# Two-layer hybrid decoder trunk on one core: layer 2's norm factors on four columns, layer 1's out projection with a block between, gate slices and y by four tiles

## The chip, the cores and the metric

The kernel runs on one core of a Trainium2 chip. The time is what the device takes for one execution of the whole program, in microseconds (us). A core has five engines with an instruction queue each: TensorE (PE; its weight loads are listed apart, as PEld), VectorE (DVE), ScalarE (ACT), GpSimd (POOL) and SyncE (SP), which here only issues DMAs. Each runs its queue in order, and waits on semaphores of the others. Matmuls write to PSUM, all else lies in SBUF or in DRAM. "Granted clock" is the TensorE clock that the throttle allowed, 1.00 being full speed.

## The reference

1024 tokens of width 1024, two layers. Layer 1 is forgetting attention (FoX: causal attention of 16 heads of 64 with a decay added to the scores), layer 2 three dilated window attentions whose results are mixed by their log-sum-exp. What bears on this change is the frame around the two mixers:

```python
def rms_norm(x, g):
    return x * lax.rsqrt(jnp.mean(x * x, axis=-1, keepdims=True) + EPS) * g

def fox_mixer(h, w_in, b_f, q_g, k_g):
    proj = h @ w_in
    q, k, v = ...                      # q and k normed by head
    gate = proj[..., 3 * INNER:4 * INNER]
    c = jnp.cumsum(jax.nn.log_sigmoid(f_logit), axis=1)
    return fox_attention(q, k, v, c), gate

for i in range(DEPTH):                 # DEPTH = 2: FoX, then dilated windows
    h = rms_norm(x, norm_g[i])
    o, gate = fox_mixer(h, ...) if i == 0 else dsw_mixer(h, ...)
    x = x + (o * jax.nn.silu(gate)) @ w_out
```

All is float32, and each large product is made of three f16 matmuls (high times high, high times low, low times high part), which keeps its accuracy.

## The kernel before, in words

**Layer 1's attention** goes by head pair (`hp`, 8 of them, two heads of 64 side by side) and query tile (`t`, 8 of 128 tokens). `fox_tile` writes one such tile: `score` makes the scores in PSUM, from which DVE makes p, ACT the exponentials and the transposed f16 parts (`ptt`, through a DMA); `values` multiplies by V into `o`; `finish` divides and gates: `rec` is the reciprocal of the softmax sum, and y = o * rec * gate for each of the two heads (L1158). The gates were projected at the start of the program and lie in DRAM (`gs_d`). In `score`, each tile loads its gate slice, 128 tokens by 128 columns (`gsf`, L1106), and `finish` stores y of the same shape to `y_d` (L1162). `turn_y` later loads rows of `y_d` back (`yt`) and PE transposes them (`transpose_rows`) for the out projection: k tiles 0 to 3, then 4 to 6. The last head pair's y (k tile 7) goes from SBUF to a transposition of its own (`turn_last`; L729 on PE, then ACT's cast to xh, L734, and DVE's remainder xl, L735).

**Layer 1's out projection** is `project_t`: the result is transposed, 128 output columns by 512 tokens in one PSUM tile `pj`. The 1024 columns come in three parts (`PARTS`, h = 0, 1, 2 with 384, 256 and 384 columns, so 3, 2 and 3 tiles m of 128), the tokens in two blocks b of 512. One such tile, a unit here, is 24 matmuls: 8 k tiles by 3. In part 0 the three units of a block are interleaved, with k tiles 0 to 3 first, then 4 to 6, then 7. Each part has a weight block of its own (`next_block` plans its loads, its bound, its scale and its `split` into f16 parts; the split's DVE step is L660, 128x768, 4 per block, one of which can go to POOL). Part 0 of both blocks stands between the last attention tiles; parts 1 and 2 follow.

**What is done with a unit** is `grown`: load the input's tile `xr`, add the projection times its weight scale (L1241), store the new x (`x1_d`) and the new x times layer 2's gain (`xn_d`), and add its square to `sacc`, by ACT, POOL and for the last unit of a block DVE. After a block's eighth unit `factors` makes layer 2's norm factor of its 512 tokens: one f32 matmul with a matrix of ones, 128x512, sums the squares over the partitions and leaves the sum in every row (`so`, L1262); DVE and ACT make 1/sqrt of it on all 128x512 values, in `fv` and `fy` in SBUF. `take` loads two tiles of `xn_d` back, multiplies by the factor (`xs`, L1275, DVE), casts to xh (ACT) and subtracts to xl (L1280, DVE for one and POOL for the other), and stores `xs` for later. Layer 2's gate projection (L694) reads xh and xl, block 0's tokens first. L904 is DVE's `peak` there, which reads the projected gates from PSUM.

**What sets the order.** The Python code says which instruction comes when in ticks: `flow.tick()` advances while matmuls are written, and `flow.at(tick, f)` writes work in at a tick; `CFG` holds the ticks for the weights' steps (`out`, `gate`), for `take` and for others. On top of it `plan_engines` and `order_engines` write a fixed order for each engine from a model of the durations: PE keeps the order of the program as far as the model calls its operands ready, DVE, ACT, POOL and SP go by the latest start that the model gives. On the chip each engine then takes that order as it is.

**Buffers.** `ps_pj` and `ps_s` have 3 PSUM tiles each, `ps_o` has 2. `n2k` is a tag of 2 KB tiles with `nb` = 3 buffers, used by `xr`, by the squares and gains of layer 1's beginning and the like; `gsl` has 3 gate slices in layer 1, `qs` 5 buffers.

Of the kernel before, what the change touches and what calls it, by code (L numbers as in the profile page):

```python
# [437 lines left out]
def trunk(ctx, tc, ins, out, cfg):  # L438
# [260 lines left out]
    def project_t(seq, done):  # L699
# [2 lines left out]
        todo = []
        for b, h in seq:
            n = PARTS[h][1] // P
            ms = [[m] for m in range(n)] if h else [list(range(n))]
            for mm in ms:
                for ks in [range(KT)] if h else [range(4), range(4, KT - 1), range(KT - 1, KT)]:
                    todo.extend((b, h, m, k) for m in mm for k in ks)
        n, s0 = 4 * NT * len({h for _, h in seq}), flow.now
        ps, ws = {}, {}  # L710
        for i, (b, h, m, k) in enumerate(todo):
            if h == 0:
                assert all((t, (k > 3) + (k > 6)) in turned for t in range(4 * b, 4 * b + 4)), (b, k, turned)
            if h not in ws:
                ws[h] = next_block(*cfg["out"][len(seq) > 2, len(ws)])
            if k == 0:
                ps[m] = ps_pj.tile([P, 512], F32, name="pj", tag="pj")
            for x, (j, a) in enumerate(((0, yh), (0, yl), (1, yh))):
                nc.tensor.matmul(ps[m], ws[h].slab(k, j)[:, m * P : (m + 1) * P], a[:, k, 512 * b : 512 * (b + 1)], start=(k == 0 and x == 0), stop=(k == KT - 1 and x == 2))  # L719
# [369 lines left out]

    def fox_tile(hp, t, kts, vt, sl):  # L1090
# [11 lines left out]
        def score(e, c):  # L1102
            a, b = pieces[c]
            if e == 0 and c == 0:
                gs = st["gs"] = lay([P, P], F32, name="gsf", tag="gsl")
                nc.sync.dma_start(gs, gs_d[t * P : (t + 1) * P, hp * P : (hp + 1) * P])  # L1106
# [45 lines left out]
        def finish():  # L1152
# [3 lines left out]
            y = sb.tile([P, P], F32, name="y", tag="y")  # L1156
            for e in range(2):
                nc.vector.scalar_tensor_tensor(y[:, e * HD : (e + 1) * HD], o[:, e, :HD], rec[:, e : e + 1], st["gs"][:, e * HD : (e + 1) * HD], ALU.mult, ALU.mult)  # L1158
# [100 lines left out]
    def factors(b):  # L1259

        so = ps_o.tile([P, 512], F32, name="so", tag="o")
        nc.tensor.matmul(so, ones.bitcast(F32), acc[:, b], start=True, stop=True)  # L1262
# [302 lines left out]
```

## Time and profile before

| | us |
|---|---|
| time, median of 3 runs | 1655.86 (1652.52 to 1656.51) |
| the profiled execution | 1656.83 |
| its span in the trace | 1654.8 |
| PE busy | 1605.9 |
| DVE busy | 1192.6 |
| ACT busy | 1063.5 |
| POOL busy | 963.9 |

The span is from the first to the last instruction of the profiled execution. Busy times are sums over an engine's instructions, by the trace; in a row of the trace x is a count, and `[0.74 <-DMA ptt<-ph]` says that the engine stood idle for 0.74 us ahead of this row, and that what it waited for last was the DMA that writes `ptt` from `ph`. `out<-in` are the program's names of the tiles, without their numbers. A name can be the buffer's: y (in `transpose_rows` the row to transpose) is `y` before the change. A row in the view by stage shows a stretch of time, the busy time of each engine in it (with the count of instructions), the granted clock, the share of the 16 DMA engines, and GB/s.

### The profile page before, as it was taken

How to read it: one execution, taken by the hardware profiler on the slowest of the kernel's cores; microseconds unless marked ns; L12 is line 12 of the kernel's file. 1: busy time of each engine (PE TensorE's matmuls, PEld its weight loads, DVE VectorE, ACT ScalarE, POOL GpSimd, SP SyncE). 2: the span in 40 equal slices, each digit the busy share in tenths (PEclk: the TensorE clock that was granted, in tenths of full speed). 3: DMA queues.
4: the chain of work that ended last, by engine and by line, in shares of the span. 5: the costliest groups of instructions: out<-in, count | busy, mean ns of one | idle time of the engine just before them, and what ended most of it. 6: DMA issues, size and time to landing. Idle time of an engine off the chain costs nothing.

```text
span 1654.8 us, 37873 instructions
## 1 busy us (share of the span) xinstructions
PE 1605.9 (97%) x13342; PEld 1037.5 (63%) x13342; DVE 1192.6 (72%) x3663; ACT 1063.5 (64%) x2746; POOL 963.9 (58%) x1252
## 2 busy tenths in 40 slices
PE   6999999999998999999999999999999999999999
PEld 4766667777664456566666666666666666666644
DVE  7757878888786586576767787777677877768751
ACT  7656778878776476566766687566566665666630
POOL 7315778778765241255555666667576766858430
PEclk9999999999999999999999999999999999999999
DMA  7335999999999884257876796768787586767952
GB/s 257 127 107 121 205 205 216 203 208 197 206 220 218 237 250 153 85 138 151 168 150 149 164 227 147 174 158 181 160 164 165 141 191 155 170 160 167 219 166 96
DMA packets 646479, 288.66 MB, mean 174 GB/s; under 512 B 493825, under 2 KB 610561, under 8 KB 646289
## 3 DMA queue, kind: packets, MB, share of 16 engines
q1 hardware_dynamic: 646288, 286.25, 74.5%
q8 instruction: 104, 1.70, 0.4%
q14 instruction: 87, 0.70, 0.1%
HBM read 124.35 MB, written 41.22 MB: 100 GB/s over the span
## 4 chain that ended last, share of the span: by engine, by line
PE 74%; DVE 10%; DMA 6%; ACT 4%; issue 3%; POOL 2%; SPq 0%; DVEq 0%; POOLq 0%; ACTq 0%
PE pj L694 56%; PE pj L719 7%; PE s L870 6%; DMA qk_t<-hl 3%; DVE w L660 2%; DVE p L1125 1%; PE ob L929 1%; PE ob L927 1%; PE ob L928 1%; DMA ptt<-ph 1%; ACT w L659 1%; PE o L929 1%; PE o L927 1%; PE o L928 1%; DVE xl L1280 1%
## 5 line engine op out<-in xcount | busy, mean ns | idle before, releaser
L694 PE MATMUL pj<-w,xh 128*128 128x384 f16 (+2 forms) x4864 | 1172.9, 324 | 6.0 <-DVE peak L904 4.3
L694 PE MATMUL pj<-w,xl 128*128 128x384 f16 (+2 forms) x2432 | 787.8, 324 | 5.2 <-DVE xl L1280 3.6
L694 PEld LDWEIGHTS <-xh 128*128 128x128 f16 x4864 | 468.1, 98 | 282.2 <-issue 8.2
L694 PEld LDWEIGHTS <-xl 128*128 128x128 f16 x2432 | 238.2, 98 | 157.5 <-DVE xl L1280 5.3
L1363 POOL TENSOR_TENSOR ph<-p,ph 128x768 f16<-128x768 f32 (+2 forms) x96 | 157.7, 1642 | 137.6 <-ACT ph L1362 130.1
L919 POOL TENSOR_TENSOR ph<-p,ph 128x512 f16<-128x512 f32 (+3 forms) x176 | 173.0, 1003 | 56.9 <-issue 37.5
L837 POOL TENSOR_TENSOR hl<-u,hl 128x512 f16<-128x512 f32 x128 | 150.9, 1179 | 53.6 <-ACT hl L836 44.9
L719 PE MATMUL pj<-xh,w 128*128 128x512 f16 x512 | 157.7, 381 | 6.2 <-DVE xr L1241 2.8
L870 PE MATMUL s<-qk_t 128*128 128x128 f16 (+1 forms) x1248 | 151.2, 238 | 6.8 <-DMA qk_t<-hl 5.1
L660 DVE SCALAR_TENSOR_TENSOR w<-raw,sws,w 128x768 f16<-128x768 f32 x96 | 146.6, 1528 | 11.0 <-ACT w L659 10.7
L794 ACT ACTIVATE sq<-pj 128x256 f32<-128x256 f32 x256 | 96.4, 377 | 86.5 <-DVE u L789 85.7
L789 DVE TENSOR_TENSOR u<-pj,gr 128x256 f32<-128x256 f32 x256 | 106.9, 418 | 45.8 <-PE pj L694 44.0
L913 ACT ACTIVATE p<-p,acc 128x512 f32<-128x512 f32 (+2 forms) x192 | 110.0, 608 | 38.0 <-DVE acc L1125 37.5
L719 PEld LDWEIGHTS <-w 128*128 128x128 f16 x768 | 74.5, 98 | 89.5 <-issue 9.2
L1352 ACT ACTIVATE p<-p,og 128x128 f32<-128x128 f32 (+1 forms) x256 | 104.1, 442 | 27.3 <-DVE og L1350 26.2
L927 PEld LDWEIGHTS <-ptt 128*128 128x128 f16 x1136 | 105.9, 98 | 19.8 <-DMA ptt<-ph 7.9
L928 PEld LDWEIGHTS <-ptt 128*128 128x128 f16 x1136 | 105.2, 96 | 11.4
L629 ACT ACTIVATE jk<-raw 128x768 f16<-128x768 f32 (+2 forms) x88 | 72.2, 820 | 62.5 <-DMA raw<-in_w_dsw 38.7
L821 POOL TENSOR_TENSOR ra<-u,cs 128x128 f32<-128x128 f32 x96 | 44.8, 467 | 108.5 <-DVE u L789 106.6
L1350 DVE CUSTOM_DVE_ANT_0 p<-s,band 128x256 f32<-128x256 f32 (+1 forms) x256 | 90.7, 373 | 22.8 <-PE s L870 22.6
L836 ACT CAST hl<-u 128x512 f16<-128x512 f32 x128 | 78.7, 614 | 42.5 <-DVE u L834 40.2
L929 PEld LDWEIGHTS <-ptt 128*128 128x128 f16 x1136 | 105.4, 97 | 0.0
(211 smaller groups left out, 3017.1 us busy)
## 6 DMA issues: line engine op xcount, KB each, us to landing
...
bc<-c_d SPq DMA_DIRECT2D x32, 256.0 KB, 4.2
...
xt<-in_xt SPq DMA_DIRECT2D x16, 256.0 KB, 3.7
gsf<-gs_d SPq DMA_DIRECT2D x64, 64.0 KB, 2.5
```

Of the source, the lines that this page charges most:

```text
L660: nc.vector.scalar_tensor_tensor(w[:, 1, :, :n], raw, self.sw, w[:, 0, :, :n], ALU.mult, ALU.subtract)
L694: nc.tensor.matmul(ps[:, :n], a[:, k, cols], w.slab(k, j), start=(k == 0 and i == 0), stop=(k == KT - 1 and i == 2))
L719: nc.tensor.matmul(ps[m], ws[h].slab(k, j)[:, m * P : (m + 1) * P], a[:, k, 512 * b : 512 * (b + 1)], start=(k == 0 and x == 0), stop=(k = ...
L789: nc.vector.tensor_mul(u[:, t % 2].rearrange("p (a b) d -> p a b d", a=2), ps[:, : 4 * HD].rearrange("p (a b d) -> p a b d", a=2, b=2), gr ...
L837: nc.gpsimd.tensor_sub(hl[:, :, :4, 1], u, hl[:, :, :4, 0])
L870: nc.tensor.matmul(s[:, c0 : c0 + cnt * P].rearrange("p (c s) -> p c s", c=cnt), q, kk[:, j : j + cnt, e], start=(h == 0), stop=(h == 1), ...
L913: nc.scalar.activation(p, p, AF.Exp, bias=acc, scale=-1.0)
L919: (nc.gpsimd if pool_l else nc.vector).tensor_sub(ph[:, e, 1, cols], p, ph[:, e, 0, cols])
L927: nc.tensor.matmul(o[:, e, :], hi, vt[:, j, e, HD:], start=(b == 0), stop=False, skip_group_check=True)
L928: nc.tensor.matmul(o[:, e, :HD], hi, vt[:, j, e, :HD], start=False, stop=False, skip_group_check=True)
L929: nc.tensor.matmul(o[:, e, :], lo, vt[:, j, e, HD:], start=False, stop=(b == n - 1), skip_group_check=True)
L1363: nc.gpsimd.tensor_sub(ph[:, 1], st["p"], ph[:, 0])
```

## The change

1. **Norm factors on four columns.** `factors` makes the sum of squares with four matmuls of 128x1, with the squares as the stationary operand, so that the 512 sums stand as 128 tokens by 4 columns. 1/sqrt is made on 128x4 values. Four DVE products put these columns on the diagonals of four 128x128 squares (`fy`), and one f32 matmul with ones (L1278, 128x512) spreads them over all partitions into a PSUM tile (`fb`), which `take`'s products now read.
2. **Out projection with a block between.** `project_t` takes a list of units with their k tiles, and can be called again with the PSUM tiles and weights that it holds. Its order is now: part 0 of block 0; part 0 of block 1 with k 0 to 3; first unit of part 1 of block 0; part 0 of block 1 with k 4 to 6; second unit of part 1 of block 0; part 0 of block 1 with k 7; then part 2 of block 0, parts 1 and 2 of block 1. The two units of part 1 stand in `ps_s`. The ticks given to the three pieces are 24, 13 and 51 where they were 32 and 64; the `take` ticks and that of `rotary_tables` move with them.
3. **Gate slices and y by four tiles.** One load brings the gate slices of four query tiles (256 KB, tag `n2k`, now 4 buffers), y is written in place of the gate, and one store takes four tiles of y to `y_d`, except for head pair 6 (by tile) and 7 (transposed from SBUF). Loads of slices go from 64 to 16, stores of layer 1's y from 56 to 20. Tag `gsl` goes from layer 1, and `qs` has 6 buffers.

```diff
+    CUTS = range(4), range(4, KT - 1), range(KT - 1, KT)
...
-    def project_t(seq, done):
+    def project_t(units, done, keys=((),), ticks=32, held=None, first=0):
...
-        todo = []
-        for b, h in seq:
-            n = PARTS[h][1] // P
-            ms = [[m] for m in range(n)] if h else [list(range(n))]
-            for mm in ms:
-                for ks in [range(KT)] if h else [range(4), range(4, KT - 1), range(KT - 1, KT)]:
-                    todo.extend((b, h, m, k) for m in mm for k in ks)
-        n, s0 = 4 * NT * len({h for _, h in seq}), flow.now
-        ps, ws = {}, {}
+        todo = [(b, h, m, k) for b, h, ms, ks in units for m in ms for k in ks]
+        n, s0 = ticks, flow.now
+        ps, ws = held or ({}, {})
...
-                ps[m] = ps_pj.tile([P, 512], F32, name="pj", tag="pj")
+                ps[h, m] = (ps_s.tile([P, 512], F32, name="pj", tag="s") if h == first > 0 else ps_pj.tile([P, 512], F32, name="pj", tag="pj"))
...
+    rows4 = {}
+
+    def four(d, hp, h):
+        return d.rearrange("(h j p) c -> h p j c", j=4, p=P)[h][:, :, hp * P : (hp + 1) * P]
...
-                gs = st["gs"] = lay([P, P], F32, name="gsf", tag="gsl")
-                nc.sync.dma_start(gs, gs_d[t * P : (t + 1) * P, hp * P : (hp + 1) * P])
+                if (hp, t // 4) not in rows4:
+                    gs = rows4[hp, t // 4] = [sb.tile([P, 4, P], F32, name="gsf", tag="n2k", bufs=cfg["nb"]), 0]
+                    nc.sync.dma_start(gs[0], four(gs_d, hp, t // 4))
...
-            y = sb.tile([P, P], F32, name="y", tag="y")
+            ys = rows4[hp, t // 4]
+            y = ys[0][:, t % 4]
             for e in range(2):
-                nc.vector.scalar_tensor_tensor(y[:, e * HD : (e + 1) * HD], o[:, e, :HD], rec[:, e : e + 1], st["gs"][:, e * HD : (e + 1) * HD], ALU.mult, ALU.mult)
+                ye = y[:, e * HD : (e + 1) * HD]
+                nc.vector.scalar_tensor_tensor(ye, o[:, e, :HD], rec[:, e : e + 1], ye, ALU.mult, ALU.mult)
+            ys[1] += 1
...
-            else:
+            elif hp == NHP - 2:
                 nc.sync.dma_start(y_d[t * P : (t + 1) * P, hp * P : (hp + 1) * P], y)
+            elif ys[1] == 4:
+                nc.sync.dma_start(four(y_d, hp, t // 4), ys[0])
...
-        nc.tensor.matmul(so, ones.bitcast(F32), acc[:, b], start=True, stop=True)
-        v, a = (lay([P, 512], F32, name="fv", tag="p") for _ in range(2))
-        y = fac2[b] = lay([P, 512], F32, name="fy", tag="qk_t")
-        nc.vector.tensor_scalar(v, so, 1.0 / D, EPS, ALU.mult, ALU.add)
+        for j in range(4):
+            nc.tensor.matmul(so[:, j : j + 1], acc[:, b, j * P : (j + 1) * P], ones.bitcast(F32)[:, :1], start=True, stop=True)
+        v, a, y = (sm.tile([P, 4], F32, name="fv", tag=f"fv{i}", bufs=2) for i in range(3))
+        nc.vector.tensor_scalar(v, so[:, :4], 1.0 / D, EPS, ALU.mult, ALU.add)
         inv_sqrt(y, v, 1, a)
+        dg = lay([P, 4, P], F32, name="fy", tag="p")
+        for j in range(4):
+            nc.vector.tensor_scalar(dg[:, j], ident, y[:, j : j + 1], None, ALU.mult)
+        fac2[b] = ps_o.tile([P, 512], F32, name="fb", tag="o")
+        nc.tensor.matmul(fac2[b], ones.bitcast(F32), dg.rearrange("p j c -> p (j c)"), start=True, stop=True)
...
-    project_t([(0, 0), (1, 0)], grown)
+    held = {}, {}
+    project_t([(0, 0, range(3), k) for k in CUTS] + [(1, 0, range(3), CUTS[0])], grown, cfg["out"][:1], 24, held, 1)
+    project_t([(0, 1, [0], range(KT)), (1, 0, range(3), CUTS[1]), (0, 1, [1], range(KT)), (1, 0, range(3), CUTS[2])], grown, cfg["out"][1:2], 13, held, 1)
     s0 = flow.now
-    flow.at(s0 + 14, rotary_tables)
+    flow.at(s0, rotary_tables)
...
-    project_t([(0, 1), (0, 2), (1, 1), (1, 2)], grown)
+    project_t([(b, h, [m], range(KT)) for b, h in ((0, 2), (1, 1), (1, 2)) for m in range(PARTS[h][1] // P)], grown, cfg["out"][2:], 51, held)
```

The order that the planner writes moves at three places. **PE, last attention tile** (tile 7 of head pair 7; `o` its values, `pt` the transposition of its y, `pj` units of the projection, `w` their weights). Before:

```order
L929 MATMUL o_9291<-vt_7432,ptt_9136 128x65
L729 MATMUL pt_9375<-ident_88,y_9357 128x128
L601 LDWEIGHTS ones_b_119
L601 MATMUL ws_9444<-vb_9442,ones_b_119 128x4
L719 LDWEIGHTS w_7789
L719 MATMUL pj_9159<-xh_101,w_7789 128x512
```

Now:

```order
L715 LDWEIGHTS w_7626
L715 MATMUL pj_9086<-xh_101,w_7626 128x512
L725 MATMUL pt_9219<-ident_88,gsf_8437 128x128
L715 LDWEIGHTS w_8763
L715 MATMUL pj_9254<-xh_101,w_8763 128x512
L715 LDWEIGHTS w_8763
L715 MATMUL pj_9254<-xl_102,w_8763 128x512
```

The transposition stood right behind the values, with the projection that needs it behind it; now it stands behind k 4 to 6 of block 1's part 0 and ahead of the second unit of part 1 (`pj_9254`), whose 24 matmuls need nothing of it. **DVE, the same place** (`rec` and the two products of y for tile 7, the splits L660 of part 2's weights, the adds of `grown`). Before:

```order
L1155 RECIPROCAL rec<-o 128x2
L1158 SCALAR_TENSOR_TENSOR y<-o,rec,gsf 128x64 x2
...
L735 SCALAR_TENSOR_TENSOR xl<-pt,sy,xh 128x128
L652 TENSOR_SCALAR ws_f<-ws_f,sy 128x1
L653 RECIPROCAL ws_f<-ws_f 128x1
L660 SCALAR_TENSOR_TENSOR w<-raw,ws_f,w 128x768 x3
L1241 SCALAR_TENSOR_TENSOR xr<-pj,ws_f,xr 128x512 x5
```

Now:

```order
L1157 RECIPROCAL rec<-o 128x2
L660 SCALAR_TENSOR_TENSOR w<-raw,ws_f,w 128x768
L1162 SCALAR_TENSOR_TENSOR gsf<-o,rec,gsf 128x64
L660 SCALAR_TENSOR_TENSOR w<-raw,ws_f,w 128x768
L1162 SCALAR_TENSOR_TENSOR gsf<-o,rec,gsf 128x64
L1248 SCALAR_TENSOR_TENSOR xr<-pj,ws_f,xr 128x512
L660 SCALAR_TENSOR_TENSOR w<-raw,ws_f,w 128x768
L731 SCALAR_TENSOR_TENSOR xl<-pt,sy,xh 128x128
L1248 SCALAR_TENSOR_TENSOR xr<-pj,ws_f,xr 128x512 x4
```

Three splits stood behind tile 7's y, in one piece; now they stand between its steps. **PE, block 0's norm factor.** Before, the sum stood 68 matmuls ahead of the projection's end. Now:

```order
L715 MATMUL pj_9634<-xh_101,w_9248 128x512
L1270 MATMUL so_9521<-ones_117,sacc_8395 128x1 x4
L715 LDWEIGHTS w_9248
...
L715 MATMUL pj_9698<-xh_101,w_9248 128x512
L1278 MATMUL fb_9540<-fy_9535,ones_117 128x512
L715 LDWEIGHTS w_9264
```

The sum stands 56 matmuls ahead of the end, and the spreading product 26 behind it, 30 ahead of the end. Behind the gates' start layer 2's instructions keep their order.

More of the change, by code (lines that the diff above doesn't have):

```diff
@@ L697, in project @@
         return ps
[L699 removed]
+    def project_t(units, done, keys=((),), ticks=32, held=None, first=0):
         under["ps"] = None
[L702 to L710 removed]
+        todo = [(b, h, m, k) for b, h, ms, ks in units for m in ms for k in ks]
+        n, s0 = ticks, flow.now
+        ps, ws = held or ({}, {})
+        keys = list(keys)
         for i, (b, h, m, k) in enumerate(todo):
@@ L714, in project_t @@
             if h not in ws:
-                ws[h] = next_block(*cfg["out"][len(seq) > 2, len(ws)])
+                ws[h] = next_block(*keys.pop(0))
             if k == 0:
-                ps[m] = ps_pj.tile([P, 512], F32, name="pj", tag="pj")
+                ps[h, m] = (ps_s.tile([P, 512], F32, name="pj", tag="s") if h == first > 0 else ps_pj.tile([P, 512], F32, name="pj", tag="pj"))
             for x, (j, a) in enumerate(((0, yh), (0, yl), (1, yh))):
-                nc.tensor.matmul(ps[m], ws[h].slab(k, j)[:, m * P : (m + 1) * P], a[:, k, 512 * b : 512 * (b + 1)], start=(k == 0 and x == 0), stop=(k == KT - 1 and x == 2))
+                nc.tensor.matmul(ps[h, m], ws[h].slab(k, j)[:, m * P : (m + 1) * P], a[:, k, 512 * b : 512 * (b + 1)], start=(k == 0 and x == 0), stop=(k == KT - 1 and x == 2))
             if k == KT - 1:
-                done(b, PARTS[h][0] // P + m, ps[m], ws[h].inv)
+                done(b, PARTS[h][0] // P + m, ps[h, m], ws[h].inv)
             while (flow.now - s0) * len(todo) < n * (i + 1):
@@ L1505, in trunk @@
     for h in range(len(PARTS)):
-        project_t([(0, h), (1, h)], finished)
+        project_t([(b, h, ms, k) for b in range(2) for ms, k in ([([m], range(KT)) for m in range(PARTS[h][1] // P)] if h else [(range(3), k) for k in CUTS])], finished)
     flow.drain()
@@ L1509, in trunk @@
     layer["cm"].__exit__(None, None, None)
[L1512 removed]
+CFG = dict(out=((), ((18, 20, 22, 24), (0, 0, 1, 1), 3, (4, 6, 8, 10)), ((18, 20, 22, 24), (14, 15, 17, 18), 24, (33, 35, 37, 39))), take=(((20, 21, 24, 27), 29), ((49, 50, 53, 56), 58)), rush=2000, gate=(((6, 7, 8, 9), (0, 0, 1, 1), 4, (5, 6, 7, 9)), ((44, 45, 46, 47), (26, 28, 30, 32), 36, (38, 40, 42, 44)), ()), bc=((1, 0, 26), (1, 1, 28), (0, 0, 38), (0, 1, 46)), wpool=3, rbufs=8, most=(0, 2), lcm=7, ps=0, pv=100, ph_=100, ph=1, wbufs=8, pl=3, um=3, lpf=8, lsd=((16, 16), (16, 14), (14, 11)), ty2=((0, 4), (1, 5)), hb=2, ub=2, qb=1, nb=4, fox=(((0, 0, 2, 2), (2, 4)), ((0, 0), (4, 4))), due=(29, 33, 39, 45, 35, 41, 49, 57), l1=dict(ga=8, ptt=4, ph=3, p=4, qk_t=6, qs=6, vt=3), l2=dict(ga=4, cmb=4, gsd=4, ptt=3, ph=3, p=2, qk_t=3, og=3, vt=3, gsl=3, par=1), wload=(18, 20, 22, 24), wbound=(0, 1, 3, 4), wscale=8, wsplit=(10, 16, 22, 12))
 def host_layout(inputs):
```

1 line of the change is left out of this document (removed).

## Prediction

> **What bounds the kernel now.** I read the page first, then busy time by stage, then TensorE's (PE's) own waits in order of time.
>
> ```profile
> span 1654.8 us, 37873 instructions
> PE 1605.9 (97%) x13342; PEld 1037.5 (63%) x13342; DVE 1192.6 (72%) x3663; ACT 1063.5 (64%) x2746; POOL 963.9 (58%) x1252
> ```
>
> PE works 97% of the span, so only its 48.9 us of idle time and its clock can give anything; faster work on DVE or SP pays only where PE waits for it. By stage (length, busy time of PE, PEld, DVE, ACT, POOL, then granted clock, DMA share, GB/s):
>
> ```profile
> 140.00:479.00 339.00, 331.09 (x3587) 236.13 (x3586) 280.30 (x917) 260.37 (x645) 262.79 (x325) 1.00 0.98 201
> 479.00:545.00 66.00, 57.33 (x528) 33.97 (x527) 39.58 (x111) 42.05 (x85) 34.89 (x39) 0.97 0.99 219
> 545.00:650.00 105.00, 99.25 (x574) 56.27 (x573) 76.86 (x152) 64.67 (x111) 33.94 (x26) 0.98 0.73 217
> ```
>
> The attention stage (140 to 479) leaves PE 7.9 us idle. The stretch the change rewrites, from the out projection's start to layer 2's first gate tiles (479 to 650), leaves 8.7 + 5.8 = 14.4 us. These rows (start, length, and in brackets idle time and its releaser) are nearly all of that:
>
> ```profile
> 501.82 0.30 PE L729 MATMUL pt<-ident,y 128*128 128x128 f32 x1 [3.16 <-DVE y L1158]
> 530.03 0.20 PE L927 MATMUL o<-vt,ptt 128*128 128x65 f16 x1 [0.74 <-DMA ptt<-ph]
> 531.81 0.30 PE L729 MATMUL pt<-ident,y 128*128 128x128 f32 x1 [0.87 <-DVE y L1158]
> 532.56 0.81 PE L719 MATMUL pj<-xh,w 128*128 128x512 f16 x3 [0.45 <-ACT xh L734]
> 537.50 0.52 PE L719 MATMUL pj<-xh,w 128*128 128x512 f16 x1 [2.83 <-DVE xr L1241]
> 594.04 0.34 PE L694 MATMUL pj<-w,xl 128*128 128x384 f16 x1 [0.71 <-DVE xl L1280]
> 598.47 0.34 PE L694 MATMUL pj<-w,xl 128*128 128x384 f16 x1 [1.98 <-DVE xl L1280]
> 624.68 0.48 PE L694 MATMUL pj<-w,xh 128*128 128x384 f16 x2 [0.77 <-DVE peak L904]
> 629.09 0.34 PE L694 MATMUL pj<-w,xl 128*128 128x384 f16 x1 [0.95 <-DVE xl L1280]
> 631.20 0.48 PE L694 MATMUL pj<-w,xh 128*128 128x384 f16 x2 [1.29 <-DVE peak L904]
> ```
>
> Two of these waits also cost clock (the last 1.00 or 0.50 but two columns from the end):
>
> ```profile
> 500.00:504.00 4.00, 2.18 (x45) 2.01 (x46) 3.53 (x10) 2.46 (x6) 1.27 (x2) 1.00 0.97 224
> 539.00:541.00 2.00, 2.00 (x6) 0.76 (x5) 0.00 (x0) 1.47 (x3) 1.07 (x1) 0.50 1.15 345
> 600.00:602.00 2.00, 2.00 (x8) 0.86 (x6) 1.14 (x2) 0.78 (x2) 0.49 (x1) 0.50 0.00 0
> ```
>
> After the 2.83 us wait (it ends at 537.50) the clock is 0.50 up to 541: 3.5 us at half speed, 1.7 us lost. After the 1.98 us wait the same again. After the 3.16 us wait it stayed at 1.00.
>
> **The change part by part.** All sums are against this execution.
>
> *Step 1, the wait of 3.16 us.* DVE's rows ahead of it and at the later waits:
>
> ```profile
> 499.18 0.29 DVE L850 TENSOR_SCALAR qs<-qk_t 64x256 int32<-64x256 int32 x1 [2.28 <-DMA qk_t<-hl]
> 500.41 0.28 DVE L1158 SCALAR_TENSOR_TENSOR y<-o,rec,gsf 128x64 f32<-128x64 f32 x1 [0.94 <-DMA gsf<-gs_d]
> 533.91 2.88 DVE L660 SCALAR_TENSOR_TENSOR w<-raw,ws_f,w 128x768 f16<-128x768 f32 x3 [0.42 <-ACT w L659]
> 536.70 2.06 DVE L1241 SCALAR_TENSOR_TENSOR xr<-pj,ws_f,xr 128x512 f32<-128x512 f32 x3
> ```
>
> Two late DMAs stand there: qk_t until 499.18, the gate slice until 500.41. The slice of four tiles is now loaded once and far ahead for tile 3, so 0.94 us goes. The qk_t wait stays; it stands behind fewer DMAs in SP's queue, which is worth some tenths. I take -1.5, bounds -3.2 (all of it) and 0 (qk_t alone sets it).
>
> *Step 2, around the last tile's values (0.74 + 0.87 + 0.45 = 2.06 us).* How often PE starts a matmul of this projection:
>
> ```profile
> 577.19 0.38 PE L719 MATMUL pj<-xl,w 128*128 128x512 f16 x1
> 577.40 0.59 PE L719 MATMUL pj<-xh,w 128*128 128x512 f16 x2
> 577.84 0.38 PE L719 MATMUL pj<-xl,w 128*128 128x512 f16 x1
> ```
>
> Three start in 0.65 us (577.19 to 577.84), 0.216 each. Ahead of the last value products PE now has about 15 more projection matmuls (3.2 us), because the first 128 columns of part 1 of block 0 stand between; that covers 0.74. Behind them come 9 matmuls (1.9 us), then tile 7's transposition, then 24 matmuls (5.2 us), which cover the copy to xh and xl (0.45). But DVE's order now puts two of part 2's weight splits (L660, 2.88/3 = 0.96 each) between the reciprocal and tile 7's two y products, 0.28 each: y comes 0.2 + 0.96 + 0.28 + 0.96 + 0.28 = 2.7 us after the values, against 1.9 us of cover plus signalling. About 1.0 us of waiting stays. Net -1.1, bounds -2.1 and +0.5 (if the weights' loads are late, y waits behind the split).
>
> *Step 3, the wait of 2.83 us and its clock.* Before, PE needed a PSUM tile whose reader xr (L1241) stood behind those three splits. Now the splits lie ahead of tile 7's y, and 24 matmuls separate them from the last pieces of block 1. Between block 1's first tile and the next unit remain 6 matmuls, 1.3 us, against one xr (2.06/3 = 0.69) and two signals: no wait from DVE. The loads of xr can still hold it: SP issues them only behind the store of part 1's first unit, so the landing of the one that counts is near the moment it is needed. I leave 0.5 us. With a gap that short the clock stays. Net -(2.83 + 1.7 - 0.5) = -4.0, bounds -4.5 and -1.0 (a wait of 1.8 us with the clock loss again).
>
> [...] Here 2.83 and 1.98 us halved it and 3.16 us did not. [...]
>
> *Step 4, block 0's norm at the gates' start (0.71 + 1.98 us).*
>
> ```profile
> 576.33 1.02 PE L1262 MATMUL so<-sacc,ones 128*128 128x512 f32 x2
> 583.07 4.81 DVE L1275 TENSOR_TENSOR xs<-xs,fy 128x512 f32<-128x512 f32 x4
> 589.50 2.47 DVE L1275 TENSOR_TENSOR xs<-xs,fy 128x512 f32<-128x512 f32 x2
> 594.56 1.82 DVE L1275 TENSOR_TENSOR xs<-xs,fy 128x512 f32<-128x512 f32 x2
> L997 DVE TENSOR_TENSOR xt<-xt,nb 128x512 f32<-128x512 f32 x16 | 10.6, 680 | 2.0 <-PE nb L967 1.9
> 122.08 0.28 PE L601 MATMUL pj<-yg,ones 128*128 128x1 f32 x2
> 122.22 0.32 PE L694 MATMUL pj<-w,xh 128*128 128x384 f16 x1
> 122.38 0.32 PE L694 MATMUL pj<-w,xl 128*128 128x384 f16 x1
> ```
>
> On DVE and ACT the chain shrinks: eight short steps, each shorter than the 0.28 of y's row, and four diagonal products. But PE keeps the order it is given: the sum stands 68 matmuls before the projection's end now, 56 after, and the spreading product 26 behind it, 30 (6.5 us) before the end. So the eight products of xs start 6.5 - 0.86 - 0.2 = 5.4 us before the end, where they start 8.9 us before it now (576.33 + 0.86 + 68 x 0.216 = 591.9, less 583.07): 3.5 us later. Reading the factor from PSUM they take 8 x 0.68 = 5.4 us (nearest row, L997) for 4.81 + 2.47 + 1.82 = 9.1: 3.7 us back. The two cancel; ACT's casts behind them do not change. I take 0, bounds -2 and +3.
>
> *Step 5, block 1's norm (0.77 + 0.95 + 1.29 us).*
>
> ```profile
> 604.57 1.02 PE L1262 MATMUL so<-sacc,ones 128*128 128x512 f32 x2
> 613.80 2.49 DVE L1275 TENSOR_TENSOR xs<-xs,fy 128x512 f32<-128x512 f32 x4
> ```
>
> The sum stands at 604.57 and its products at 613.80, 9.2 us behind; they come 0.56 + 26 gate matmuls at 0.16 (122.22 to 122.38) + 0.86 + 0.2 = 5.8 after, 3.4 us sooner. The 0.95 goes, and half of the two waits for peak, which stands behind xs and xl on DVE. Net -2.0, bounds -3.0 and 0.
>
> *Step 6, PE's added work.* The sum took 0.86 us (576.33 to 577.19); four with one column, 0.14 each (122.08 to 122.22), take 0.56, and the spreading product, as wide as the old sum, 0.86: +0.56 a block, +1.1 in all.
>
> *Step 7, the gate slices and y in the attention stage.*
>
> ```profile
> L1106 SPq DMA_DIRECT2D gsf<-gs_d x64: 399/430/1592, 138.8 to 518.9; - x64
>   DMA y_d<-y: 5.2, 6
>   DMA gsf<-gs_d: 1.4, 2
> gsf<-gs_d SPq DMA_DIRECT2D x64, 64.0 KB, 2.5
> xr<-in_xp SPq DMA_DIRECT2D x16, 256.0 KB, 3.5
> ```
>
> 64 loads become 16 and 56 stores 20: 84 issues of some 0.4 us leave SP's queue, where the transposes stand that PE waits for, and DVE's 5.2 us for a free y go. The bytes, and so the DMA share of 0.98, stay. PE has only 7.9 us idle here: I take -1.0, bounds -3 and the first rival.
>
> Sum: -1.5 - 1.1 - 4.0 + 0 - 2.0 + 1.1 - 1.0 = **-8.5 us**: span 1646.3, and with the 2.0 us around it (1656.83 less 1654.8) 1648.3 for such a run. That run lay 1.0 us above the median, so **1647.5** for a median. Adding the terms' half-widths as independent gives about 5 us: 1642 to 1653 is the forecast's own range.
>
> **The rivals.** *Late four-tile loads (slower).* The first tile of each of the 16 groups now needs 256 KB, which lands in 3.5 us (the row of xr) against 2.5; its y waits on DVE, in order, and behind it stand the score products that PE waits for. At 1.0 us each, 14 groups inside the attention stage cost 14 us, and it ends at 1661; from 0.6 us each on PE the gain is gone. For it: DVE is busy 280 of 339 us, and the second half's load is issued only behind tile 4's transposes. Against it: only 2 of 64 loads were waited for, 1.4 us in all. [...]
>
> *The gates' start takes it back (no change).* If step 4 is +4, because the spreading product comes late and ACT's casts follow it, and step 5 gives nothing, the sum is -8.5 + 4 + 2 = -2.5: 1653.4.
>
> *Everything closes.* If all 14.4 us and both clock losses (3.4) go, less step 6: -16.7, 1639.
>
> **How the numbers follow.** Forecast 0.55, loads 0.13, gates' start 0.22, everything 0.10. To hold 8 in 10 the range reaches to the last and to most of the first rival: 1640 to 1659. 0.3%, 5 us, is about what a measurement can tell: faster (below 1651) 0.47 + 0.10 + 0.01 = 0.58; same 0.08 + 0.20 + 0.02 = 0.30; slower 0.12.
>
> **What would show it.** Step 1: tile 3's transposition waits under 2 us. Steps 2 and 3: at the last tile one wait near 1 us for y, none above 1 us for xr, and the clock 1.00 to the gates. Step 4: waits for xl at the gates of 2 to 3 us in all; over 5 us is the second rival. Step 5: xl of block 1 no longer waited for. Step 7: DVE's waits for gsf stay below 3 us in sum; more, with PE idle above 8 us in the attention stage, is the first rival. The forecast is wrong if PE's idle time between the projection's start and the gates is not below 9 us.

## The result and the profile after

The changed kernel takes 1637.38 us (median of 5, 1637.3 to 1640.53) beside 1653.54 for the kernel before (median of 5): 0.9898 of it, 95% interval 0.9881 to 0.9915, 16.2 us less. Timed again beside other runs of the kernel before it was 0.9886 (0.9866 to 0.9906). The forecast was 8.5 us less, 1647.5 in a range of 1640 to 1659; the case "everything closes" had 1639 and a chance of 0.10. Of the 10.1 us between the forecast and the measured median, 2.3 are the kernel before, whose median is 1653.54 here and was 1655.86 there.

The page of the changed kernel, its span and its engines:

```profile
span 1638.8 us, 37766 instructions
PE 1602.5 (98%) x13358; PEld 1037.7 (63%) x13358; DVE 1191.2 (73%) x3671; ACT 1059.5 (65%) x2746; POOL 959.5 (59%) x1252
```

PE's busy time fell by 3.4 us, its idle time by 12.6. To see where, both traces are cut at the same places of the program: the first score matmul, the projection's first matmul, the first gate matmul of layer 2, some 280 gate matmuls later, and the last start on PE. Busy time by stage, with the columns of the prediction (length, PE, PEld, DVE, ACT, POOL, clock, DMA share, GB/s); the kernel before:

```profile
141.60:479.30 337.70, 329.79 (x3580) 235.48 (x3579) 279.79 (x915) 259.41 (x642) 262.91 (x324) 1.00 0.98 201
479.30:591.90 112.60, 103.93 (x742) 54.94 (x741) 72.77 (x178) 67.07 (x126) 50.29 (x51) 0.98 0.92 228
591.90:640.00 48.10, 42.35 (x275) 26.91 (x274) 38.66 (x70) 32.97 (x59) 17.34 (x14) 0.96 0.75 222
640.00:1651.10 1011.10, 1001.12 (x7937) 635.63 (x7935) 702.76 (x2248) 615.26 (x1721) 578.60 (x783) 1.00 0.70 160
```

and the changed kernel:

```profile
141.50:474.60 333.10, 329.43 (x3581) 235.37 (x3580) 284.25 (x916) 258.41 (x641) 262.58 (x325) 1.00 0.98 205
474.60:582.70 108.10, 102.78 (x749) 55.11 (x747) 70.17 (x184) 65.27 (x127) 46.82 (x50) 1.00 0.95 241
582.70:625.20 42.50, 41.14 (x281) 27.14 (x280) 33.48 (x73) 32.70 (x58) 16.77 (x14) 1.00 0.78 238
625.20:1634.40 1009.20, 1000.80 (x7939) 635.97 (x7936) 705.33 (x2249) 614.26 (x1721) 578.00 (x783) 1.00 0.69 160
```

The attention stage became 4.6 us shorter, the projection 4.5, the gates' start 5.6, the rest of layer 2, whose order is the same, 1.9. The clock is 1.00 in all four stages. PE's waits above 0.6 us between 475 and 640 in the changed kernel:

```profile
480.30 0.28 PE L866 MATMUL s<-qk_t,qs 128*128 128x256 f16 x1 [0.61 <-DVE qs L846]
496.64 0.27 PE L866 MATMUL s<-qk_t 128*128 128x256 f16 x1 [1.31 <-DVE xl L731]
529.23 0.30 PE L725 MATMUL pt<-ident,gsf 128*128 128x128 f32 x1 [0.64 <-DVE gsf L1162]
564.15 0.16 PE L601 MATMUL ws<-vb,ones_b 128*128 128x4 bf16 x1 [1.15 <-POOL vb L640]
568.88 1.05 PE L1270 MATMUL so<-ones,sacc 128*128 128x1 f32 x8 [1.31 <-DVE sacc L1261]
585.41 0.34 PE L695 MATMUL pj<-w,xl 128*128 128x384 f16 x1 [0.73 <-POOL xl L1292]
```

Tile 3's 3.16 us and the xr wait of 2.83 us are gone, tile 7 is left with 0.64; new are a wait for a weight bound on POOL and one of the sum of squares for its last add. At the gates' start 0.73 us is the longest. From the projection's start to the end of the gates' start PE is idle for 6.7 us, where it was 14.4; the forecast's sign of being wrong was 9 or more.

### The profile page after: what moved, and what is told of

Read it like the earlier page. It is cut to its first block, busy times and chain, and to the rows that moved or that the text cites. A ratio compares the mean times of both kernels' runs of the same rounds, so it can differ in the third digit from the quotient of the medians.

```text
span 1638.8 us, 37766 instructions
## 1 busy us (share of the span) xinstructions
PE 1602.5 (98%) x13358; PEld 1037.7 (63%) x13358; DVE 1191.2 (73%) x3671; ACT 1059.5 (65%) x2746; POOL 959.5 (59%) x1252
## 4 chain that ended last, share of the span: by engine, by line
PE 79%; DVE 7%; DMA 5%; ACT 4%; issue 2%; POOL 1%; SPq 1%; DVEq 0%; ACTq 0%; POOLq 0%
PE pj L695 60%; PE s L866 6%; PE pj L715 6%; DMA qk_t<-hl 3%; DVE w L660 2%; PE ob L925 1%; PE ob L923 1%; PE ob L924 1%; PE o L925 1%; PE o L923 1%; PE o L924 1%; DVE p L1127 1%; DVE qs L846 1%; DMA yt<-y_d 1%; ACT w L659 1%
## 5 line engine op out<-in xcount | busy, mean ns | idle before, releaser
L660 DVE SCALAR_TENSOR_TENSOR w<-raw,sws,w 128x768 f16<-128x768 f32 x96 | 150.0, 1564 | 9.5 <-ACT w L659 9.2
L923 PEld LDWEIGHTS <-ptt 128*128 128x128 f16 x1136 | 106.0, 98 | 13.4 <-DMA ptt<-ph 1.5
L817 POOL TENSOR_TENSOR ra<-u,cs 128x128 f32<-128x128 f32 x96 | 44.8, 467 | 108.7 <-DVE u L785 105.8
```

What stands on the lines that cost most here:

```text
L660: nc.vector.scalar_tensor_tensor(w[:, 1, :, :n], raw, self.sw, w[:, 0, :, :n], ALU.mult, ALU.subtract)
L923: nc.tensor.matmul(o[:, e, :], hi, vt[:, j, e, HD:], start=(b == 0), stop=False, skip_group_check=True)
```

## The experiments

The table comes first. Ratios are to the kernel before, run beside each; the three lengths are PE's stages as above, from one profiled execution each (in us; attention, projection, gates' start; a dash where no cut was made).

| kernel | ratio (95%) | stages |
|---|---|---|
| before | 1 | 337.7, 112.6, 48.1 |
| changed kernel | 0.9898 (0.9881 to 0.9915) | 333.1, 108.1, 42.5 |
| e9: again | 0.9886 (0.9866 to 0.9906) | 331.2, 107.7, 42.6 |
| e1: norm alone | 0.9974 (0.9958 to 0.9990) | 336.4, 111.4, 43.5 |
| e2: order alone | 1.0007 (0.9995 to 1.0019) | 335.3, 109.4, 51.2 |
| e3: rows by four alone | 0.9958 (0.9944 to 0.9973) | 330.8, 111.2, 48.1 |
| e4: without norm | 0.9937 (0.9922 to 0.9951) | 330.7, 106.0, 50.1 |
| e7: without order | 0.9930 (0.9910 to 0.9950) | 330.9, 112.6, 43.3 |
| e8: without rows | 0.9974 (0.9959 to 0.9990) | 336.8, 113.9, 47.1 |
| e5: stores by tile | 0.9925 (0.9902 to 0.9948) | 336.0, 111.8, 42.5 |
| e6: loads by tile | 0.9923 (0.9901 to 0.9945) | 333.3, 107.5, 42.3 |
| e16: both by tile | 0.9966 (0.9952 to 0.9979) | 348.9, 109.4, 43.1 |
| e12: qs 5 | 0.9891 (0.9872 to 0.9911) | 332.4, 107.7, - |
| e10: n2k 3 buffers | 0.9932 (0.9912 to 0.9952) | 330.6, 111.1, 47.4 |
| e15: n2k 3, xr in ga | 0.9900 (0.9886 to 0.9914) | 333.5, 108.3, 44.0 |
| e13: without rows, xr in ga | 0.9932 (0.9919 to 0.9945) | 337.4, 108.7, 43.8 |
| e14: xr in ga | 0.9906 (0.9894 to 0.9919) | 333.9, 109.5, - |
| e11: factor in SBUF | 0.9935 (0.9916 to 0.9955) | 332.4, 105.8, 48.8 |

The rest of layer 2 has the same order in all of them and lay between 1007 and 1013 us: so much can differ there without an edit.

**e1, the norm alone.** The hunks of `factors` put into the kernel before:

```diff
-        nc.tensor.matmul(so, ones.bitcast(F32), acc[:, b], start=True, stop=True)
+        for j in range(4):
+            nc.tensor.matmul(so[:, j : j + 1], acc[:, b, j * P : (j + 1) * P], ones.bitcast(F32)[:, :1], start=True, stop=True)
...
+        fac2[b] = ps_o.tile([P, 512], F32, name="fb", tag="o")
```

> The kernel before with part 1 of the change alone (norm factors on four columns, spread into PSUM). The prediction priced it apart: in the order of before the sum keeps its place, so xs starts at most 1 us later than before or sooner (the short chain), and its products save 3.7 us; steps 4 and 5 without the later place of the spreading product, less the added work of 1.1 us. Theory A (each part works in its own stage): the waits for xl at the gates fall from 0.71 + 1.98 us to below 1 us, the half clock of 1.7 us there goes, block 1's 3.0 us fall by 2 or more: -5 us, about 1648.5 against a before of 1653.5. Rival B (the gates' gain of the whole change came from the new order of the out projection): waits for xl stay above 2 us, and the time moves by less than 2 us.

0.9974: 4.3 us of 1655 less. The gates' start is 4.6 us shorter, and the last of its two waits is

```profile
594.41 0.34 PE L694 MATMUL pj<-w,xl 128*128 128x384 f16 x1 [0.77 <-DVE xl L1285]
```

beside 0.90 for xh: theory A in size and place.

**e2, the order alone.** The hunks of `project_t`, its calls and the ticks put into the kernel before:

```diff
-    project_t([(0, 0), (1, 0)], grown)
+    project_t([(0, 0, range(3), k) for k in CUTS] + [(1, 0, range(3), CUTS[0])], grown, cfg["out"][:1], 24, held, 1)
...
-    flow.at(s0 + 14, rotary_tables)
+    flow.at(s0, rotary_tables)
```

> The kernel before with part 2 alone (out projection with a block between, its ticks and the take ticks). Theory A: the waits of 3.16 us (tile 3's y) stays, those around tile 7 and for xr (0.74 + 0.87 + 0.45 + 2.83 us, and 1.7 us of half clock) shrink to 1.5 us: -5 us; the gates' start stays as before or gets worse by 0 to 3 us, as the sum stands later: in all -2 to -5 us, 1649 to 1651. Rival B (this part carries most of the 16 us, at the gates too): -10 us or more, waits for xl below 1.5 us in sum. Rival C (parts only work together, since the planner writes another order with each): within 2 us of before.

Nothing is gained. The waits around tile 7 and the xr wait of 2.83 us are gone as the prediction had it, but another for xr comes nearly 40 us later, and the gates' start takes the rest back (two waits of PE, and the two microseconds at half clock that follow the second):

```profile
573.92 0.39 PE L715 MATMUL pj<-xh,w 128*128 128x512 f16 x1 [2.25 <-DVE xr L1237]
590.68 0.50 PE L695 MATMUL pj<-w,xl 128*128 128x384 f16 x1 [4.28 <-DVE xl L1276]
...
594.00:596.00 2.00, 2.00 (x8) 0.92 (x7) 2.00 (x3) 1.52 (x3) 1.29 (x1) 0.50 1.05 316
```

That is the second rival, "the gates' start takes it back", in the kernel that lacks the short norm. Neither theory A's 2 to 5 us nor rival B's 10 came; C's number did, and the runs below show why.

**e3, the rows by four alone** (the hunks of `rows4`, with n2k 4 and qs 6):

```diff
-                nc.sync.dma_start(gs, gs_d[t * P : (t + 1) * P, hp * P : (hp + 1) * P])
...
+                    nc.sync.dma_start(gs[0], four(gs_d, hp, t // 4))
...
+            elif ys[1] == 4:
+                nc.sync.dma_start(four(y_d, hp, t // 4), ys[0])
```

> The kernel before with part 3 alone (gate slices and y by four tiles, n2k 4 buffers, qs 6). Theory A: PE's idle time in the attention stage falls from 7.7 us to about 3.6 us as in the changed kernel, tile 3's 3.16 us go or shrink to 1.5: -5 to -7 us, 1646.5 to 1648.5. The prediction's steps 1 and 7 gave -2.5 us. Rival C (the attention stage's gain comes with the planner's other order or from one profile to the next): idle time in the attention stage stays above 6 us and the time moves by less than 3 us.

7.0 us less by the ratio, all of it in the attention stage:

```profile
141.60:472.40 330.80, 328.76 (x3581) 235.84 (x3580) 288.01 (x916) 258.16 (x641) 262.59 (x325) 1.00 0.99 206
529.22 0.38 PE L719 MATMUL pj<-xh,w 128*128 128x512 f16 x1 [2.83 <-DVE xr L1252]
```

PE is idle there for 2.0 us where it was for 7.9; the xr wait stands as it was, so nothing of step 3 came with this part. Theory A.

**e4, the change without the norm** (the first hunk above taken back):

```diff
-        for j in range(4):
-            nc.tensor.matmul(so[:, j : j + 1], acc[:, b, j * P : (j + 1) * P], ones.bitcast(F32)[:, :1], start=True, stop=True)
+        nc.tensor.matmul(so, ones.bitcast(F32), acc[:, b], start=True, stop=True)
```

> The changed kernel without part 1 (wide norm factors in SBUF again, new order and rows by four kept). Theory A: as the sum now stands 56 and not 68 matmuls ahead of the projection's end and the products of xs cost 9.1 us again, waits for xl at the gates' start rise to 4 us or more, with half clock behind them, and block 1's 3 us are back: 1637.4 + 6 = 1643 to 1646. Rival B (the order carries the gates' gain): 1637 to 1640, waits for xl below 2 us.

1644.46: the gates' start is 7.6 us longer than in the changed kernel, the projection 2.1 us shorter. Theory A; the order of the projection doesn't carry the gates.

**e5 to e6 and e16, what in the rows' part counts.** e5 stores y by query tile, e6 loads the slices by query tile into the quarters of the tile of four, e16 does both; y in place, n2k 4 and qs 6 stay.

```diff
-            elif hp == NHP - 2:
+            else:
                 nc.sync.dma_start(y_d[t * P : (t + 1) * P, hp * P : (hp + 1) * P], y)
-            elif ys[1] == 4:
-                nc.sync.dma_start(four(y_d, hp, t // 4), ys[0])
```

```diff
-                    nc.sync.dma_start(gs[0], four(gs_d, hp, t // 4))
+                nc.sync.dma_start(rows4[hp, t // 4][0][:, t % 4], gs_d[t * P : (t + 1) * P, hp * P : (hp + 1) * P])
```

> The changed kernel, but y is stored by query tile again (56 stores; loads by four and y in place of the gate kept, so DVE needs no free y). In the kernel before, SP's queue stood 16.8 us in 35 waits of the y stores for DVE in the attention stage, and the transposes of hl and ph behind them in that queue. Theory A (the gain of the attention stage is SP's queue, held by stores of y): PE's idle time in the attention stage is back at 5 to 8 us and the time at +3 to +4 us over the changed kernel, 1640.5 to 1642. Rival B (it was DVE's wait for a free y, 5.2 us, which this kernel doesn't have): within 1.5 us of the changed kernel's 1637.4, idle time below 4.5 us.

> The changed kernel, but the gate slices are loaded by query tile, each into its quarter of the tile of four (64 loads; stores by four kept). Loads wait for nothing but a free buffer, once in four. Theory A (stores of y held SP's queue): the attention stage's idle time stays at 2 to 4.5 us, the time within 2 us of the changed kernel. Rival C (the number of issues in SP's queue counts, some 0.4 us each): 48 more issues are 19 us more of SP's queue, idle time back at 5 to 8 us and +3 us or more, as much as stores by tile give.

> The changed kernel with both loads of slices and stores of y by query tile (64 and 56 again), y in place, n2k 4, qs 6 kept: what is left of the rows' part without its fewer transfers. Theory A (SP's queue is what the rows relieve, by stores that wait and by issues; each half gave back about 5 us by the medians): 0.994 to 0.996, attention idle 5 to 8 us. Rival (y in place and buffers carry the rows' gain, the halves' losses were half noise): 0.990 to 0.992.

By the ratios either half alone costs about 5 us, with intervals that touch the changed kernel's; by the stages e5 costs 3 to 5 us of attention and 3.7 of the projection, e6 0 to 2 us. e6's profiled execution was the fastest of its six (1641.37, their median is 1645.47), so between "loads by tile cost nothing" and "5 us" this stays open. Both together lose more than the part alone had brought: e16's ratio is 0.7 to 0.8% above the changed kernel's, 11 to 13 us, where e3 had gained 7.0. The attention stage of e16 (its row by stage, and its two longest waits for DMAs) is

```profile
141.80:490.70 348.90, 332.65 (x3569) 235.37 (x3567) 282.57 (x910) 256.68 (x636) 261.76 (x323) 0.99 0.96 193
331.77 0.20 PE L923 MATMUL o<-vt,ptt 128*128 128x65 f16 x1 [2.59 <-DMA ptt<-ph]
464.63 0.29 PE L866 MATMUL s<-qk_t 128*128 128x128 f16 x1 [2.53 <-DMA qk_t<-hl]
```

longer than before, with projection and gates near the changed kernel's (this execution lay 4.0 us above the median of e16's twelve; its longest wait, 4.3 us, is one of PE for DVE). So y in place, the buffers and qs bring nothing by themselves; the gain comes only with the fewer transfers. Why e16 is longer in this stage than the kernel before, which moves its slices and its y by tile too, no run shows.

What the stores do in SP's queue shows in its own waits (line and what it waited for, us in total, times, longest); the kernel before has nine such groups for the y stores, 16.8 us in 33 waits (the 35 of e5's expectation count two of other transfers), of which the largest are

```profile
SPq L1162 <- DVE y L1158: 5.0, 7, 1.4
SPq L1162 <- DVE rec L1155: 3.6, 5, 1.6
```

In e16 the same sum, the waits of the y stores for DVE in the attention stage, is 22.6 us, in e5 13.7, in e6 4.9 and in the changed kernel 4.7. PE's waits for the transposed `ptt` in that stage, in the kernel before and in the changed one, are

```profile
PE o L927 <- DMA ptt<-ph: 4.1, 4, 1.5
PE o L923 <- DMA ptt<-ph: 0.4, 1, 0.4
```

and 6.5 us in e16. Behind such stores in SP's queue stand the transposing DMAs for qk_t and ptt. In the kernel before, DVE's second product of a y ends at 316.13, the store of y is issued at 316.16 (0.75 us) and the transposition of ptt behind it at 317.02, where POOL's ph ahead of it had ended at 316.55. That this is the way in which the transfers cost PE is read from these sums; no run took the queue's waits away by themselves, and it is not the only way. The longest of PE's four waits before has another chain behind it (one row of POOL, one of PE):

```profile
221.88 0.45 POOL L1122 TENSOR_TENSOR bc<-bc,band 128x128 f32<-128x128 f32 x1 [2.25 <-DMA bc<-c_d]
226.15 0.20 PE L927 MATMUL o<-vt,ptt 128*128 128x65 f16 x1 [1.47 <-DMA ptt<-ph]
```

Here the transposition waited for POOL's `ph`, and POOL had waited 2.25 us for a load of `bc` out of the same queue. SP as a whole is not short of time: its waits for POOL in the stage rose from 130 us to 179, about what 84 issues of 0.43 us and the stores' 12 us had taken. What seems to count is when a single transposition or load gets its turn.

**e12, qs at 5 buffers.**

```diff
- ... qs=6 ...
+ ... qs=5 ...
```

> The changed kernel with qs at 5 buffers, as before. Theory A (the sixth qs is a minor part of the attention stage's gain, which is the SP queue's): the time within 1.5 us of the changed kernel's, attention idle below 4.5 us. Rival (qs is what PE waits for when qk_t comes late, and carries the gain): attention idle 5 us or more, +3 us or more.

0.9891 beside e9's 0.9886, with PE idle for 3.4 us in the attention stage: the sixth buffer does nothing that can be measured.

**e7 and e8, the change without the order and without the rows** (the hunks of e2 and of e3 taken back, with e3's n2k and qs):

> The changed kernel without part 2 (parts 1 and 3, out projection in the order of before). Rows by four alone gave 0.9958 and the norm alone 0.9974, the order alone 1.0007 with 4.28 us of wait for xl and half clock at the gates' start. Theory A (the order saves its 5 us at the last attention tile, and pays them at the gates' start unless the norm is short): waits of about 2.8 us for xr and 0.87 + 0.45 + 0.7 us at tile 7 with half clock are back, gates' start below 2 us: ratio 0.993, 1642 to 1644 beside 1637.4. Rival (the order is worth nothing, the sum of the two others makes it): ratio 0.9898 to 0.991, as the whole change.

> The changed kernel without part 3 (parts 1 and 2). Theory A (parts 1 and 2 together are worth 4.3 us of the norm and 5 us of the order, and the attention stage keeps its 5 to 8 us of idle time): ratio 0.994 to 0.995, the time 8 to 10 us below before; gates' start with less than 2.5 us of waits for xl, no half clock there. Rival (the order needs the early rows by four to get its gain, as tile 3's y waits for its gate slice): ratio 0.997 or more, with 3 us of wait for tile 3's y and xr waits kept.

e7 has 0.9930, what e1 and e3 give together (0.9974 x 0.9958 = 0.9932); the order adds 0.3 to 0.4% to that, about 6 us, and nothing to e1 alone (e8, 0.9974, with PE waiting 2.58 us for a weight bound and at half clock behind it, 0.50 from 578 to 584). So the order needs something that the rows' part brings.

**e10, n2k at 3 buffers.**

```diff
- ... nb=4 ...
+ ... nb=3 ...
```

> The changed kernel with n2k at 3 buffers, as before. The order alone and with the norm kept waits for xr (2.25 us) or late starts there, and gained nothing (1.0007, 0.9974), while with the rows' part it gained 3.4 to 5.3 us. Theory A (the order needs the fourth buffer of n2k, which the rows' part brings along: an xr load no longer waits for ACT's reading of an earlier xr): waits for xr of 2 us or more come back in the projection, its length goes from 108.2 to 110 to 112 us, ratio 0.992 to 0.994. Rival (the fourth buffer is for the gate slices, the order gains because the attention ahead of it ends earlier): projection within 1 us of 108.2, any loss is in the attention stage. Rival 2 (it does nothing): ratio as the changed kernel beside it.

It is the buffer. The ratio goes to 0.9932, as without the order at all. Two of PE's waits in e10, and one of SP's queue between 520 and 560:

```profile
535.63 0.38 PE L715 MATMUL pj<-xh,w 128*128 128x512 f16 x1 [1.76 <-ACT xg L1251]
580.08 1.12 PE L1278 MATMUL fb<-fy,ones 128*128 128x512 f32 x2 [1.74 <-DVE fy L1276]
...
SPq L1246 <- DMA x_d<-xr: 3.0, 2, 1.8
```

The load of an xr (L1246) stands in the queue until the store of an earlier xr has landed; the changed kernel has no such wait. Everything of `grown` follows late: the PSUM tile that PE needs, the squares, and the factor, which PE now waits 1.74 us for.

**e15 and e13, xr in other buffers.** `grown` takes xr from the 8 buffers of tag ga, which the attention has nearly done with: in e15 with n2k at 3, in e13 in parts 1 and 2 without the rows.

```diff
-        xr = sb.tile([P, 512], F32, name="xr", tag="n2k", bufs=cfg["nb"])
+        xr = lay([P, 512], F32, name="xr", tag="ga")
```

> The changed kernel with n2k at 3 buffers (0.9932) and xr in ga's buffers. Theory A (the loss with 3 was xr's): back at 0.9886 to 0.990. Rival (it was the gate slices', three tiles of four in place of four): 0.992 to 0.994 as with 3 buffers.

> Parts 1 and 2 without the rows by four (0.9974 with n2k at 3 buffers), but with xr of the out projection in the 8 buffers of another tag (ga, which is nearly free there), so that xr's loads have buffers as with the rows' part. Theory A (the order's gain hangs on xr's buffers: with n2k at 3 the whole change lost 8.8 us): projection from 113.9 to 109 or less, gates' start from 47.1 to 43, ratio 0.990 to 0.9935. Rival (the order needs the earlier attention that the rows give, tile 3's y and the transposes): ratio 0.996 to 0.998, projection above 112.

e15 is back at 0.9900, so the loss with 3 was xr's and not the slices'. e13 goes from e8's 0.9974 to 0.9932 with an attention stage as before the change, and its projection is

```profile
478.80:587.50 108.70, 103.85 (x749) 54.74 (x747) 71.51 (x182) 64.88 (x126) 47.70 (x51) 1.00 0.94 244
```

0.6 us from the changed kernel's. The earlier attention is not what the order needs.

**e14, a try for a faster kernel:** the changed kernel (n2k 4) with e15's edit.

> The changed kernel with xr of the out projection in ga's 8 buffers; gate slices alone stay in n2k (4). A try for a faster kernel: in the changed kernel DVE still waits 5 us for xr's loads in the projection, and PE 0.8 to 1.3 us for sacc, which follows. Theory A (buffers of xr are still what is late): projection shorter by 1 to 2.5 us, ratio 0.987 to 0.988. Rival (with four buffers xr's loads are late for SP's queue, not for a buffer): as the changed kernel, 0.9886 to 0.9898, or slower if ga's rotation holds the loads behind the last attention tile's.

0.9906, no faster: a fifth place for xr is worth nothing. No run was faster than the changed kernel.

**e11, the factor in SBUF.**

```diff
-        fac2[b] = ps_o.tile([P, 512], F32, name="fb", tag="o")
...
+        fb = ps_o.tile([P, 512], F32, name="fb", tag="o")
...
+        fac2[b] = lay([P, 512], F32, name="fs", tag="qk_t")
+        nc.vector.tensor_copy(fac2[b], fb)
```

> The changed kernel, but the spread factor is copied from PSUM to SBUF by DVE, and the products of xs read it there. Theory A (the products got shorter, 935 to 676 ns on the mean, because with the factor in PSUM they don't share SBUF's access with POOL, whose xl ran beside the long ones): some of the 16 products take 1.2 to 1.9 us again, mean 0.85 to 0.95 us, POOL's xl go from a median of 1440 to 1800 ns, PE's waits at the gates' start rise from 1.2 to 3 us or more, +2 to +4 us. Rival (short products only come from the place in the order): mean within 0.05 us of 0.68, the time within 1.5 us of the changed kernel's.

1646.84 beside e9's 1637.16 on the same chip: this copy, and what follows from it, costs as much as the norm part gains in the changed kernel (e4). Duration (min/median/max, ns) of the steps of `take` in e11:

```profile
L1289 DVE TENSOR_TENSOR xs<-xs,fs x16: 676/684/1909, 573.4 to 611.4; 128x512 f32<-128x512 f32 x16
L1294 POOL TENSOR_TENSOR xl<-xs,xh x8: 1638/1861/2027, 575.3 to 612.7; 128x512 f16<-128x512 f32 x8
L1294 DVE TENSOR_TENSOR xl<-xs,xh x8: 1031/1675/2215, 576.8 to 614.1; 128x512 f16<-128x512 f32 x8
```

and in the changed kernel:

```profile
L1287 DVE TENSOR_TENSOR xs<-xs,fb x16: 657/676/689, 576.5 to 609.4; 128x512 f32<-128x512 f32 x16
L1292 DVE TENSOR_TENSOR xl<-xs,xh x8: 1027/1055/2135, 578.3 to 610.9; 128x512 f16<-128x512 f32 x8
L1292 POOL TENSOR_TENSOR xl<-xs,xh x8: 1427/1440/1739, 579.3 to 612.2; 128x512 f16<-128x512 f32 x8
```

With the factor in SBUF some products take up to 1909 ns and the xl of both engines are a quarter and more longer at the median; with the factor in PSUM no product takes over 689. Theory A, and more than its 2 to 4 us: the gates' start is 6.2 us longer. The planner also wrote another order of these steps on DVE, so for the time of the kernel the copy's 0.7 us, the slower steps and that order aren't told apart. For the durations they are: the same two groups in the kernel before and in e4 (old and new order, factor in SBUF), then in e1 (old order, factor in PSUM), are

```profile
L1275 DVE TENSOR_TENSOR xs<-xs,fy x16: 679/685/1909, 583.1 to 625.2; 128x512 f32<-128x512 f32 x16
L1280 POOL TENSOR_TENSOR xl<-xs,xh x8: 1513/1821/2189, 585.5 to 626.6; 128x512 f16<-128x512 f32 x8
L1282 DVE TENSOR_TENSOR xs<-xs,fy x16: 679/689/1916, 574.4 to 614.3; 128x512 f32<-128x512 f32 x16
L1287 POOL TENSOR_TENSOR xl<-xs,xh x8: 1449/1830/2222, 576.3 to 615.7; 128x512 f16<-128x512 f32 x8
L1280 DVE TENSOR_TENSOR xs<-xs,fb x16: 669/678/687, 579.9 to 616.5; 128x512 f32<-128x512 f32 x16
L1285 POOL TENSOR_TENSOR xl<-xs,xh x8: 1427/1436/1473, 583.3 to 618.6; 128x512 f16<-128x512 f32 x8
```

The longest product and POOL's median go with the place of the factor in either order. DVE's own xl don't (1102 ns at the median in e4, 1140 in e1), so their 1675 in e11 is not put down to it. In the kernel before, seven of the 16 products overlap an xl of POOL in time; four of them take 1219 to 1909 ns, the three others, and the nine that overlap none, 679 to 691. In the changed kernel eight overlap one, and none of the 16 takes over 689. That the two engines share an access to SBUF, as theory A has it, is its author's reading of these durations; no run shows the access itself.

## Why the prediction was too small

**Step 1** (-1.5): the 3.16 us went, but 0.61 and 1.31 us came back at the score matmuls beside it (0.61 and 1.11 in e3 and e4); net -1.2. Right.

**Step 2** (-1.1): 2.06 us became 0.64, -1.4; of the three waits the one for y stayed, as was said. Right.

**Step 3** (-4.0): all 4.5 us went. The size was right, and the step rested on a condition that was priced at 0.5 us for the wrong reason: the loads of xr were thought late for their place in SP's queue, and it is the fourth n2k buffer that keeps them early. Without it (e10) the whole order is worth nothing that can be measured. The change's line on buffers was given no term of its own.

**Step 4** (0) failed. These rows bear on it, the first products and the last xl of block 0 on DVE and POOL in the changed kernel, and the last xl before:

```profile
576.46 1.88 DVE L1287 TENSOR_TENSOR xs<-xs,fb 128x512 f32<-128x512 f32 x3 [0.63 <-PE fb L1278]
587.99 1.50 DVE L1292 TENSOR_TENSOR xl<-xs,xh 128x512 f16<-128x512 f32 x1 [0.62 <-ACT xh L1291]
589.02 1.73 POOL L1292 TENSOR_TENSOR xl<-xs,xh 128x512 f16<-128x512 f32 x1 [0.35 <-ACT xh L1291]
598.91 1.57 DVE L1280 TENSOR_TENSOR xl<-xs,xh 128x512 f16<-128x512 f32 x1
```

The place was nearly right: the products start 6.3 us ahead of the first gate matmul at 582.74, where 5.4 were forecast and 8.8 stood before (the forecast's rows give 8.8, not the 8.9 that it wrote). The 0.2 us that the forecast put, with no row, between the spreading product and the first of xs came (576.26, where PE's next matmul starts, to 576.46). Of the steps on 128x4 values, forecast below 0.28 us each, one took 0.94 and the others 0.15 to 0.21. The 0.68 us each for the products were right, and so was "ACT's casts behind them do not change" (1110 to 1088 ns at the median). So start and products nearly cancel, as was forecast: the chain from the first product to the last xl became 3.1 us shorter (17.4 to 14.3; POOL's four xl in it take 6.0 us in sum and took 7.9) and starts 2.5 us later, and the last xl ends 8.0 us behind the gates' start, where it was 8.6. What failed is the step from there to PE's time. The term held the waits and the clock loss at what they were; 0.71 + 1.98 us of waiting became four waits with 1.2 us in sum, none over 0.73, and the 1.7 us of half clock went too: -3.2. Why the xl come so evenly is not taken apart further. The second rival, at the same place, was real in e2 and e4, where the norm is wide, and partly in e10, where the spreading product comes late, as that rival had it (the gates' start takes 47.4 us there).

**Step 5** (-2.0): 3.0 us of waiting went, and none of it is left in that stage. The mechanism was right, the size 1.0 short, as the waits for peak went whole and not by half.

**Step 6** (+1.1): four narrow sums hold PE for 0.92 us (568.88 to the next matmul at 569.80), not 0.56, so the added work is 1.8 us. What was missed beside it: the sum now waits 1.31 us for its last square, and a weight bound 1.15 us for POOL.

**Step 7** (-1.0) failed, by the most. The attention stage gave 4.6 us in this pair of traces, beyond the bound of -3. In the ten traces with the rows by four it takes 330.6 to 333.9 us, in the five without them (before, e1, e2, e8, e13) 335.3 to 337.7: 4.8 us between the means, with PE idle for 1.9 to 4.5 us and for 5.1 to 7.9. The idle time of 7.9 us was seen, and the stores that leave SP's queue, but the gain was taken as one eighth of it by choice, not from a row. The views that bear on it, SP's own waits (16.8 us in 33 waits of the y stores for DVE) and PE's 4.1 us of waits for ptt in this stage, weren't quoted. The first rival was wrong: a load of four slices lands after 3.9 us at the median, and DVE never waits for one in the changed kernel's attention stage.

The remaining 1.9 us, in a part of layer 2 that no edit touches, lie within the spread from one execution to another.

The number of "everything closes" (16.7 us less) nearly came, but not its way, so that is luck: it had all of the gain behind the attention stage, and 4.6 us of it came inside that stage.

By e13, e10 and e7 the three parts aren't a sum: alone they are worth 4.3, 0 and 7.0 us, together 17 to 19. The order needs xr's buffers, which the rows' part brings along. Without the short norm it gives back at the gates' start 2.0 of the 5.2 us that it saves in the projection (e4 beside e3).
